# Starting every large on-chip tile of a decoder trunk at a multiple of 256 bytes

## The chip, the cores and the metric

The kernel runs on one core of a Trainium2 chip. The metric is the time of one execution on the device in microseconds (us), the median of three runs. A profile is one more execution, taken by the hardware profiler.

## What is computed

One decoder layer over 512 tokens of width 1024, all in float32, and a final norm. Cut to what matters here:

```python
h = rmsnorm(x, norm1_g)
x_rnn, g_rnn, dq, dk, dv, fq, fk, fv, f_logit, gates = split(h @ w_in)      # 1024 x 8200
y_rnn = gelu(g_rnn) * rg_lru(causal_conv4(x_rnn))                           # width 1024
lam   = exp(sum(lq1 * lk1)) - exp(sum(lq2 * lk2)) + 0.2                     # one number
y_diff = rmsnorm(diff_attention(dq, dk, dv, lam, rel_bias)) * 0.8           # 4 heads
y_fox  = forgetting_attention(fq, fk, fv, cumsum(log_sigmoid(f_logit + b))) # 8 heads
m = sum_b sigmoid(gates_b) * (y_b @ w_branch_b)
x = x + m @ w_out
u_gate, u_val = split(causal_conv3(rmsnorm(x, norm2_g) @ ffn_up))           # 1024 x 5632
x = x + (gelu(u_gate) * u_val) @ ffn_down                                   # 2816 x 1024
out = rmsnorm(x, final_g)
```

## The kernel before

Every product is a sum of three matmuls: each float32 operand is split into a high part `h` (rounded to the type float32r) and the rest `l`, and `mm3` (L81) adds h·h, h·l and l·h in a PSUM bank. A matmul reads two tiles of SBUF: the stationary one, 128 columns wide, which a weight load (PEld in the profile) puts into the array ahead of the matmul, and the moving one, as a rule 512 float32 columns (2,048 bytes in each partition). The TensorE (PE) has 4,363 matmuls, nearly all from the one line L77, and each has its own weight load.

Weights come from HBM in tiles of 128 x 1024. `load_w` (L93) puts one into a raw tile `wr`, ScalarE (ACT) casts it to `wh` (L101), VectorE (DVE) subtracts to get `wl` (L102). In the projections of the first half (`psq`, `psk`, `psx`, `psg`, `psgt`, and `psbr` for the branches) and in the FFN's first product (`psu`) `wh` and `wl` are the stationary side and an activation (`xh`/`xl`, `h2h`/`h2l`) moves; for one 128 x 512 result the order is sixteen matmuls with `wh` (each of its eight slices twice), then eight with `wl`. In the FFN's second product (`psd`) `wh`/`wl` move and the activations `acth`/`actl` are stationary. Its last weights on each half are held as pages (`wph`, `wpl`, from `load_wp`), and the product with w_out (`pswo`) moves `woh`/`wol`.

SBUF is divided into pools, laid one after the other: `const` (constants, each as long as it is), `page` (58 tiles of 2,048 bytes a partition, where most activations live), `wpool` (`wr`, `wh`, `wl`, three buffers each), `sm` (small vectors), and `apool`, which `fpool` follows in the same place (22 tiles of 2,048 bytes, for attention, later for `woh`/`wol` of the first five slices and for `acth`/`actl` of the first ten blocks). Where a pool starts follows from the length of those before it, and no pool is padded. A weight tile has 1,056 columns, since one pair of weights needs them; that is 4,224 bytes, 16 and a half times 256, so of three buffers in a row the middle one stands 128 bytes off the other two. In the built program the tiles start at these bytes past a multiple of 256:

- pages: 32
- `wr`: 32, 160, 32 (three buffers); `wh`: 160, 32, 160; `wl`: 32, 160, 32
- attention tiles: 96

Within a tile, slices start at multiples of 512 bytes, and so keep the tile's remainder.

A scheduler orders each engine's instructions when the kernel is built; an engine runs its own list in order and waits there. SyncE (SP) issues nearly all transfers. The first half interleaves eight heads of one attention and four of the other with the projections; from 475 us on the program is five long stretches, each of one kind of matmul.

Two constants matter for the change. `rows` (L160) holds the forget bias (8 columns) and the four lambda vectors (256 columns), read from HBM by one transfer at L226. `bneg` (L252) is a 4 x 128 fill of -1e30, written to a scratch tensor at L256.

Of the kernel before, what the change touches and what calls it, by code (L numbers as in the profile page):

```python
# [10 lines left out]
F32 = mybir.dt.float32  # L11
F32R = mybir.dt.float32r
AF = mybir.ActivationFunctionType
ALU = mybir.AluOpType
ADD, SUB, MUL, MAX = ALU.add, ALU.subtract, ALU.mult, ALU.max
# [9 lines left out]
NPG = 58  # L25
NAT = 22
NWARM = 9
NLAST = (2, 4)
LAM_INIT = 0.2
GELU_C = 0.7978845608028654  # L30
# [7 lines left out]
    COFF[_n] = _o  # L38
    _o += _w
NCOL = _o  # L40
ROFF = {"fbf": 0, "lam": 8}
NROW = 264

T_XR, T_GR, T_DQ, T_DK, T_FQ, T_FK, T_GT = 0, 8, 16, 20, 24, 28, 32

# [1 line left out]
def build(ctx, tc, A, out):  # L47
    nc = tc.nc
    PE, V, SC, G = nc.tensor, nc.vector, nc.scalar, nc.gpsimd

    const = ctx.enter_context(tc.tile_pool(name="const", bufs=1))
    page = ctx.enter_context(tc.tile_pool(name="page", bufs=NPG))
    wpool = ctx.enter_context(tc.tile_pool(name="wpool", bufs=3))
# [7 lines left out]
    def pg(name, dt=F32):  # L61
        return page.tile([128, 512], dt, name=name, tag="pg")

    def ag(name, dt=F32):
        return apool[0].tile([128, 512], dt, name=name, tag="at")
# [4 lines left out]
    def abank(name):  # L70
        return psa.tile([128, 512], F32, name=name, tag="at")

    def small(shape, name, bufs=None):
        return sm.tile(shape, F32, name=name, tag=name, bufs=bufs)
# [16 lines left out]
    hp = [False]  # L91

    def load_w(ap, n, parts=1):  # L93
        raw = wpool.tile([128, 1056], F32, name="wr", tag="wr")
        hi = wpool.tile([128, 1056], F32R, name="wh", tag="wh", bufs=3)
        lo = wpool.tile([128, 1056], F32R, name="wl", tag="wl", bufs=3)
        with tc.high_priority() if hp[0] else ExitStack():
            for p in range(parts):
                c = slice(n // parts * p, n // parts * (p + 1))
                nc.sync.dma_start(raw[:, c], ap[:, c])  # L100
                SC.copy(hi[:, c], raw[:, c])  # L101
                V.tensor_sub(lo[:, c], raw[:, c], hi[:, c])  # L102
        return hi, lo

    def load_wp(ap):

        raw = wpool.tile([128, 1056], F32, name="wr", tag="wr")
        nc.sync.dma_start(raw[:, :1024], ap)
        res = []
        for p in range(2):  # L110
            c = slice(512 * p, 512 * (p + 1))
            h = pg("wph", F32R)
            l = pg("wpl", F32R)
            SC.copy(h, raw[:, c])
            V.tensor_sub(l, raw[:, c], h)
            res.append((h, l))
        return res
# [39 lines left out]
    V.memset(epsc, EPS)  # L157
    pre = const.tile([128, 1], F32, name="pre")
    SC.activation(pre, epsc, AF.Exp)
    rows = const.tile([128, NROW], F32, name="rows")  # L160

    def col(n, j, w=1):
        return cols[:, COFF[n] + j:COFF[n] + j + w]
# [4 lines left out]
    pw = abank("pwarm")  # L168
    for _ in range(NWARM):
        PE.matmul(pw, warm[:, 0:128], warm, start=True, stop=True)  # L170
# [19 lines left out]
    for w in range(KD // 2):  # L190
        load_x(2 * w)
        hi, lo = load_w(A["wv_d"][w], 1024, 2)
        load_x(2 * w + 1)
        if w == 0:
            nc.sync.dma_start(cols[:, 8:], A["cols"][:, 8:])
        todo = [(t, 2 * w + kk, j) for kk in range(2) for j in range(3) for t in range(NT)]
        if w == KD // 2 - 1:
            todo.sort()
        for t, k, j in todo:
            kk = k % 2  # L200
            a, b = ((xh[k], hi), (xl[k], hi), (xh[k], lo))[j]
            mm(pst[t], a[:, 128 * t:128 * (t + 1)], b[:, 512 * kk:512 * (kk + 1)],
               k == 0 and j == 0, k == KD - 1 and j == 2)

    ss1 = const.tile([128, 2, NT], F32, name="ss1")
    for t in range(NT):
        for hf in range(2):
            xt = ag("xt")
            nc.sync.dma_start(xt, A["x"][128 * t:128 * (t + 1), 512 * hf:512 * (hf + 1)])
            SC.activation(xt, xt, AF.Square, accum_out=ss1[:, hf, t:t + 1])  # L210
    pre_w = [load_w(A["w_t"][i], 1024) for i in (T_DQ, T_DK)]
    ssum = small([128, NT], "ssum", 1)
    V.tensor_add(ssum, ss1[:, 0, :], ss1[:, 1, :])
# [9 lines left out]
    nc.sync.dma_start(flip, A["flip"])  # L223
    flr = const.tile([128, 128], F32R, name="flr")
    V.tensor_copy(flr, flip)
    nc.sync.dma_start(rows, A["rows"].partition_broadcast(128))  # L226
    relb = const.tile([32, 4], F32, name="relb")
    nc.sync.dma_start(relb, A["rel_bias"])
    oh = ag("oh")[0:32, :]
# [19 lines left out]
    PE.matmul(bps[0:4, :], relb, oh, start=True, stop=True)  # L249
    bsb = ag("bsb")[0:4, :]  # L250
    V.tensor_copy(bsb, bps[0:4, :])
    bneg = const.tile([4, 128], F32, name="bneg")  # L252
    V.memset(bneg, NEG)
    bdr = dram.tile([4, 640], F32, name="bdr")
    nc.sync.dma_start(bdr[:, 0:512], bsb)
# [3 lines left out]
    def vload_t(ap, kper, n):  # L259
        return lambda: [load_w(ap[0], kper * n), load_w(ap[1], kper * n)]  # L260
# [14 lines left out]
    def ev_fv(g):  # L275
        def ev(t, ps):
            p = pg("fv", F32R)

            pv = p.rearrange("p (u x d) -> p u x d", u=2, x=4)
            src = ps[:, 0:256].rearrange("p (u x d) -> p u x d", u=2, x=2)  # L280
            with tc.high_priority():
                for x in range(2):
                    h = pv[:, :, 3 * x, :]
                    l = pv[:, :, 1 + x, :]
                    SC.activation(h, src[:, :, x, :], AF.Copy, scale=rs1[:, t:t + 1])
                    V.scalar_tensor_tensor(l, src[:, :, x, :], rs1[:, t:t + 1], h, op0=MUL, op1=SUB)
            fv[t][g] = p
            if g == 0:
                V.scalar_tensor_tensor(flog[:, t, :], ps[:, 256:264], rs1[:, t:t + 1],
                                       rows[:, ROFF["fbf"]:ROFF["fbf"] + 8], op0=MUL, op1=ADD)  # L290
        return ev


# [13 lines left out]
        slabs.append(tl)  # L307


    lamw = rows[:, ROFF["lam"]:ROFF["lam"] + 256].rearrange("p (a b) -> p a b", a=4)  # L310
    lamp = ag("lamp")[:, 0:128].rearrange("p (a b) -> p a b", a=2)
    V.tensor_mul(lamp, lamw[:, 0::2, :], lamw[:, 1::2, :])
    lams = small([128, 2], "lams", 1)
    V.tensor_reduce(lams, lamp, axis=mybir.AxisListType.X, op=ADD)
    lame = small([128, 2], "lame", 1)
    SC.activation(lame, lams, AF.Exp)
# [489 lines left out]
    wo = [None] * KD  # L806

    def wo_load(k):
        raw = wpool.tile([128, 1056], F32, name="wr", tag="wr")
        nc.sync.dma_start(raw[:, :1024], A["w_out"][128 * k:128 * (k + 1), :])  # L810
        hl = []
        for hf in range(2):
            al = ag if k < 5 else pg
            h = al("woh", F32R)
            l = al("wol", F32R)
            SC.copy(h, raw[:, 512 * hf:512 * (hf + 1)])
            V.tensor_sub(l, raw[:, 512 * hf:512 * (hf + 1)], h)
            hl.append((h, l))
        wo[k] = hl
# [8 lines left out]
    for c in range(2, 8):  # L828
        last += gi(2, c)
        if c < 7:  # L830
            last += do(lambda c=c: wo_load(c - 2))
    for c in range(0, 8, 2):
        last += pi_(2, c)
        if c < 6:
            last += do(lambda c=c: wo_load(5 + c // 2))
# [9 lines left out]
    def up_w(idx, paged=False):  # L845
        if paged:
            pp = load_wp(A["up_t"][idx])
            return lambda k: tuple(x[:, 128 * (k % 4):128 * (k % 4 + 1)] for x in pp[k // 4])
        hi, lo = load_w(A["up_t"][idx], 1024)
        return lambda k: (hi[:, 128 * k:128 * (k + 1)], lo[:, 128 * k:128 * (k + 1)])  # L850
# [42 lines left out]
                V.scalar_tensor_tensor(h2l[k][:, ts_], src, col("g2", k), h2h[k][:, ts_], op0=MUL, op1=SUB)  # L893


    fwh = const.tile([128, 88], F32, name="fwh")
    for j in range(3):
        V.tensor_scalar(fwh[:, 22 * j:22 * (j + 1)], col("fw", 44 * j + 22, 22), 0.5, None, op0=MUL)
    V.tensor_scalar(fwh[:, 66:88], col("fb", 22, 22), 0.5, None, op0=MUL)
# [64 lines left out]
    for hf in range(2):  # L964
# [8 lines left out]

        nl = NLAST[hf]
        nxt = load_w(A["dn_t"][hf, 0], 1024)
        for p in range(NP - nl):
            hi, lo = nxt
            if p + 1 < NP - nl:
                nxt = load_w(A["dn_t"][hf, p + 1], 1024)
            else:  # L980
                held = [(p, load_wp(A["dn_t"][hf, p])) for p in range(NP - nl, NP)]
            for kk in range(2):
                for t in range(NT):
                    dmm(t, 2 * p + kk, hi[:, 512 * kk:512 * (kk + 1)], lo[:, 512 * kk:512 * (kk + 1)])
# [81 lines left out]
```

## Time and profile before

| | |
|---|---|
| median of three runs | 949.76 us (948.43 to 950.57) |
| the profiled execution, its own time | 949.56 us |
| its span, first to last instruction | 947.7 us |
| PE busy | 934.7 us, 99% of the span |
| VectorE, ScalarE, GpSimd busy | 631.7, 486.6, 112.4 us |
| granted TensorE clock, mean | 0.996 of full speed |
| read from HBM | 92.26 MB |

A matmul's duration in a row (389 to 404 ns for 512 columns) includes its filling and draining, which overlap the next matmul. What a matmul costs in a stream is the distance from its start to the next one's; the rows give it as a stretch divided by a count.

### The profile page before, as it was taken

Reading aid. Unit: us, or ns where it says so; the run is one execution under the profiler, and the core shown is the slowest. Engines: PE = TensorE matmul, PEld = TensorE weight load, DVE = VectorE, ACT = ScalarE, POOL = GpSimd, SP = SyncE. Lnnn points to the kernel's source line nnn. Section 1 sums busy time; section 2 is a strip of 40 time slices with the busy share of each in tenths; the row PEclk is TensorE's granted clock in tenths of the full one; section 3 lists DMA queues with packets and bytes.
Section 4 is the critical chain, followed back from the end, with each engine's and each line's share of the span. In section 5 each row is a group of like instructions: output and inputs, shape, how many; then the busy total and the mean of one; then the engine's idle time right before and its main releaser. Section 6 shows DMA issues by size and latency. Waiting matters only on the chain.

```text
span 947.7 us, 11817 instructions
## 1 busy us (share of the span) xinstructions
PE 934.7 (99%) x4363; PEld 770.7 (81%) x4363; DVE 631.7 (67%) x1207; ACT 486.6 (51%) x839; POOL 112.4 (12%) x85
## 2 busy tenths in 40 slices
PE   9999999999998999999999999999999999999997
PEld 6788888998886887888888889888888888888885
DVE  5779787777669889755566634877677677633323
ACT  7668776855474775434453344544444444422212
POOL 0022210200133253221210000000000000000000
PEclk9999999999999999999999999999999999999999
DMA  9622222232231323223253600323223222334112
GB/s 320 194 80 87 95 73 68 68 112 76 98 106 58 104 67 112 85 82 101 67 200 110 207 16 1 112 91 109 90 89 99 102 89 90 112 105 140 45 67 89
DMA packets 31433, 95.14 MB, mean 100 GB/s; under 512 B 3680, under 2 KB 5220, under 8 KB 31376
## 3 DMA queue, kind: packets, MB, share of 16 engines
q1 hardware_dynamic: 30800, 93.35, 29.2%
q10 hardware_dynamic: 576, 1.05, 0.3%
q8 instruction: 34, 0.56, 0.2%
q14 instruction: 23, 0.19, 0.1%
HBM read 92.26 MB, written 2.12 MB: 100 GB/s over the span
## 4 chain that ended last, share of the span: by engine, by line
PE 95%; DVE 3%; issue 1%; DMA 0%; ACT 0%; SPq 0%; POOLq 0%; POOL 0%
PE psu L77 26%; PE psgt L77 13%; PE psd L77 12%; PE psbr L77 9%; PE psg L77 6%; PE psv L77 5%; PE psx L77 5%; PE pswo L77 5%; PE psq L77 4%; PE psk L77 4%; PE pss L77 2%; PE pso L77 2%; PE pst L429 1%; DVE hh L637 1%; DVE gr L638 1%
## 5 line engine op out<-in xcount | busy, mean ns | idle before, releaser
L101 ACT CAST wh<-wr 128x1024 fp32r<-128x1024 f32 (+2 forms) x143 | 146.4, 1024 | 157.0 <-PE psu L77 55.3
L102 DVE TENSOR_TENSOR wl<-wr,wh 128x1024 fp32r<-128x1024 f32 (+2 forms) x143 | 174.1, 1217 | 75.3 <-ACT wh L101 66.7
L77 PE MATMUL psu<-h2l,wh 128*128 128x512 f32 (+1 forms) x360 | 136.9, 384 | 0.0
L77 PE MATMUL psu<-h2h,wh 128*128 128x512 f32 (+1 forms) x360 | 136.9, 383 | 0.0
L77 PE MATMUL psu<-h2h,wl 128*128 128x512 f32 (+1 forms) x360 | 87.2, 384 | 0.0
L77 PEld LDWEIGHTS psu<-h2l,wh 128*128 128x128 f32 x360 | 67.8, 188 | 14.0
L77 PEld LDWEIGHTS psu<-h2h,wh 128*128 128x128 f32 x360 | 67.8, 188 | 13.8
L77 PEld LDWEIGHTS psu<-h2h,wl 128*128 128x128 f32 x360 | 65.8, 188 | 14.4
L77 PE MATMUL psgt<-xh,wh 128*128 128x512 f32 x192 | 76.6, 399 | 0.0
L77 PE MATMUL psgt<-xl,wh 128*128 128x512 f32 x192 | 76.2, 397 | 0.0
L77 PE MATMUL psd<-wh,actl 128*128 128x512 f32 x128 | 50.2, 393 | 0.0
L77 PE MATMUL psd<-wl,acth 128*128 128x512 f32 x128 | 50.1, 391 | 0.0
L77 PE MATMUL psd<-wh,acth 128*128 128x512 f32 x128 | 49.9, 392 | 0.0
L77 PE MATMUL psgt<-xh,wl 128*128 128x512 f32 x192 | 49.1, 395 | 0.0
L864 POOL TENSOR_TENSOR rs3y<-rs3y,mhalf 128x1 f32<-128x1 f32 x4 | 2.2, 551 | 364.5 <-DVE rs3y L863 364.5
L77 PEld LDWEIGHTS psgt<-xh,wl 128*128 128x128 f32 x192 | 35.7, 188 | 8.1
L77 PEld LDWEIGHTS psgt<-xh,wh 128*128 128x128 f32 x192 | 36.1, 188 | 7.5
L77 PEld LDWEIGHTS psgt<-xl,wh 128*128 128x128 f32 x192 | 36.1, 188 | 7.5
L926 DVE SCALAR_TENSOR_TENSOR u<-gq,u 128x512 f32<-128x512 f32 x22 | 15.2, 692 | 34.1 <-ACT gq L925 34.1
L651 DVE TENSOR_TENSOR z<-psgt,rsb 128x512 f32<-128x512 f32 x24 | 16.5, 688 | 31.1 <-PE psgt L77 31.1
L906 DVE SCALAR_TENSOR_TENSOR u<-psu,cols,u 128x511 f32<-128x511 f32 (+1 forms) x44 | 32.9, 748 | 6.1 <-ACT u L903 5.3
L123 ACT CAST acth<-u 128x512 fp32r<-128x512 f32 x22 | 13.7, 621 | 43.5 <-DVE u L927 43.5
(288 smaller groups left out, 2179.6 us busy)
## 6 DMA issues: line engine op xcount, KB each, us to landing
wr<-w_t_in SPq DMA_DIRECT2D x56, 512.0 KB, 3.3
wr<-up_t_in SPq DMA_DIRECT2D x44, 512.0 KB, 3.3
wr<-dn_t_in SPq DMA_DIRECT2D x22, 512.0 KB, 3.4
wr<-br_r_in SPq DMA_DIRECT2D x8, 512.0 KB, 3.4
wr<-w_out_in SPq DMA_DIRECT2D x8, 512.0 KB, 3.9
xraw<-xT_in SPq DMA_DIRECT2D x8, 256.0 KB, 6.0
wr<-wv_d_in SPq DMA_DIRECT2D x8, 256.0 KB, 5.4
xt<-x_in SPq DMA_DIRECT2D x8, 256.0 KB, 5.4
```

The lines of the kernel that those rows point to most:

```text
L77: PE.matmul(ps, a, b, start=start, stop=stop)
L101: SC.copy(hi[:, c], raw[:, c])
L102: V.tensor_sub(lo[:, c], raw[:, c], hi[:, c])
L123: SC.copy(h, src)
L429: PE.transpose(ps[:, 128 * i:128 * (i + 1)], ws[i][:, 128 * j:128 * (j + 1)], ident)
L637: V.tensor_tensor_scan(hh, a, xc, 0.0, op0=MUL, op1=ADD)
L638: V.scalar_tensor_tensor(gr, gr, 0.5, hh, op0=MUL, op1=MUL)
L651: V.tensor_mul(z, ps, rsb)
L864: G.tensor_tensor(y, y, mhalf[:, 0:1], op=ALU.pow)
L906: V.scalar_tensor_tensor(u[:, s:], ps[:, :512 - s], w[j], u[:, s:], op0=MUL, op1=ADD)
L926: V.scalar_tensor_tensor(ug, q, 1.0, ug, op0=ADD, op1=MUL)
```

## The change

Lengths of tiles are changed so that every pool, and every tile in the pools `page`, `wpool` and `apool`/`fpool`, starts at a multiple of 256 bytes. In the built program all these tiles then stand at 0 past a multiple of 256, in place of 32, 96 and 160.

- Weight tiles get 1,088 columns (4,352 bytes, 17 times 256) in place of 1,056. The columns that are used stay the same.
- To make room, the 256 lambda columns leave `rows` and come by a transfer of their own into an attention tile `lamr`; the product of lambda vectors and `bneg` use other columns of the same tile.
- `fwh` and `lams` are made longer as padding; the added columns are not used.

No computing instruction is added or taken away; one transfer of 8 and one of 256 columns stand in for one of 264.

```diff
+WCOL = 1088
...
-ROFF = {"fbf": 0, "lam": 8}
-NROW = 264
+NFB = 8
...
-        raw = wpool.tile([128, 1056], F32, name="wr", tag="wr")
-        hi = wpool.tile([128, 1056], F32R, name="wh", tag="wh", bufs=3)
-        lo = wpool.tile([128, 1056], F32R, name="wl", tag="wl", bufs=3)
+        raw = wpool.tile([128, WCOL], F32, name="wr", tag="wr")
+        hi = wpool.tile([128, WCOL], F32R, name="wh", tag="wh", bufs=3)
+        lo = wpool.tile([128, WCOL], F32R, name="wl", tag="wl", bufs=3)
...
-    rows = const.tile([128, NROW], F32, name="rows")
+    rows = const.tile([128, NFB], F32, name="rows")
...
-    nc.sync.dma_start(rows, A["rows"].partition_broadcast(128))
+    nc.sync.dma_start(rows, A["rows"][0:NFB].partition_broadcast(128))
+    lamr = ag("lamr")
+    nc.sync.dma_start(lamr[:, 0:256], A["rows"][NFB:NFB + 256].partition_broadcast(128))
...
-    bneg = const.tile([4, 128], F32, name="bneg")
+    bneg = lamr[0:4, 384:512]
...
-    lamw = rows[:, ROFF["lam"]:ROFF["lam"] + 256].rearrange("p (a b) -> p a b", a=4)
-    lamp = ag("lamp")[:, 0:128].rearrange("p (a b) -> p a b", a=2)
+    lamw = lamr[:, 0:256].rearrange("p (a b) -> p a b", a=4)
+    lamp = lamr[:, 256:384].rearrange("p (a b) -> p a b", a=2)
...
-    lams = small([128, 2], "lams", 1)
+    lams = small([128, 24], "lams", 1)[:, 0:2]
...
-    fwh = const.tile([128, 88], F32, name="fwh")
+    fwh = const.tile([128, 144], F32, name="fwh")
```

The scheduler's lists differ in few places, all in the first 70 us or so; behind them PE, DVE, ACT and SP have the same lists as before. On SP, before, some 20 us into the execution (the constants and the relative bias table `relb`, its one-hot matrix `oh` and the scratch `bdr`):

```order
L223 DMA flip<-flip_in 128x128
L226 DMA rows<-rows_in 128x264
L228 DMA relb<-rel_bias_in 32x4
L230 DMA oh<-onehot_in 32x512
L256 DMA bdr<-bneg 4x128
L100 DMA wr<-w_t_in 128x1024 x4
```

and now:

```order
L223 DMA flip<-flip_in 128x128
L226 DMA rows<-rows_in 128x8
L228 DMA lamr<-rows_in 128x256
L230 DMA relb<-rel_bias_in 32x4
L232 DMA oh<-onehot_in 32x512
L258 DMA bdr<-lamr 4x128
L100 DMA wr<-w_t_in 128x1024 x4
```

One transfer more stands ahead of `relb`, `oh` and the weights. On DVE, before, at 26 to 42 us (`dvl` splits the first values, `bsb` takes the bias table out of PSUM, `hkl` splits its shifted copies, `lamp`, `lams` and `nlam` make lambda):

```order
L225 CAST flr<-flip 128x128
L102 TENSOR_TENSOR wl<-wr,wh 128x1024
L244 SCALAR_TENSOR_TENSOR dvl<-psv,rs_327,dvh 128x512 x2
L102 TENSOR_TENSOR wl<-wr,wh 128x1024
L251 COPY bsb<-bps 4x512
L244 SCALAR_TENSOR_TENSOR dvl<-psv,rs_327,dvh 128x512
L102 TENSOR_TENSOR wl<-wr,wh 128x1024
L124 TENSOR_TENSOR hkl<-hk,hkh 128x512 x4
L312 TENSOR_TENSOR lamp<-rows 128x128
```

and now:

```order
L225 CAST flr<-flip 128x128
L314 TENSOR_TENSOR lamr<-lamr 128x128
L102 TENSOR_TENSOR wl<-wr,wh 128x1024
L246 SCALAR_TENSOR_TENSOR dvl<-psv,rs_327,dvh 128x512
L316 TENSOR_REDUCE lams<-lamr 128x2
L246 SCALAR_TENSOR_TENSOR dvl<-psv,rs_327,dvh 128x512
L102 TENSOR_TENSOR wl<-wr,wh 128x1024
L253 COPY bsb<-bps 4x512
L246 SCALAR_TENSOR_TENSOR dvl<-psv,rs_327,dvh 128x512
L320 TENSOR_TENSOR nlam<-lame 128x1
L321 TENSOR_SCALAR nlam<-nlam 128x1
```

The four small operations of lambda come ahead of `bsb` and `hkl`; before, they came behind. PE, before, at 40 to 48 us (`psj` are the bias slabs, put between the matmuls of a projection `psx`):

```order
L77 MATMUL psj<-hkl,flr 128x512
L77 MATMUL psj<-hkh,flr 128x512
L77 MATMUL psx<-xl,wh 128x512
L77 MATMUL psj<-hkl,flr 128x512
L77 MATMUL psj<-hkh,flr 128x512
L77 MATMUL psx<-xh,wh 128x512
```

The change puts the first pair of `psj` two matmuls of `psx` later and the last pair behind the sixteenth:

```order
L77 MATMUL psx<-xl,wh 128x512
L77 MATMUL psx<-xh,wh 128x512
L77 MATMUL psx<-xl,wh 128x512
L77 MATMUL psj<-hkl,flr 128x512
L77 MATMUL psj<-hkh,flr 128x512
L77 MATMUL psx<-xh,wl 128x512 x8
```

## Rows read from the trace of the kernel before

**Rows 1.** The page: busy time, share of span, instructions; chain by engine.

```profile
PE 934.7 (99%) x4363; PEld 770.7 (81%) x4363; DVE 631.7 (67%) x1207; ACT 486.6 (51%) x839; POOL 112.4 (12%) x85
...
PE 95%; DVE 3%; issue 1%; DMA 0%; ACT 0%; SPq 0%; POOLq 0%; POOL 0%
```

**Rows 2.** PE's waits over the span: for whom, us, times, longest.

```profile
PE psbr L77 <- DVE xs L587: 3.4, 1, 3.4
PE pwarm L170 <- POOL warm L167: 1.3, 1, 1.3
PE psv L77 <- ACT wh L101: 0.8, 1, 0.8
```

**Rows 3.** PE's timeline in three neighbouring psu results: start, length, what, count.

```profile
597.91 0.39 PE L77 MATMUL psu<-h2h,wh 128*128 128x512 f32 x1
...
601.54 2.03 PE L77 MATMUL psu<-h2h,wl 128*128 128x512 f32 x8
603.41 0.40 PE L77 MATMUL psu<-h2h,wh 128*128 128x512 f32 x1
...
607.13 1.99 PE L77 MATMUL psu<-h2h,wl 128*128 128x512 f32 x8
608.97 0.40 PE L77 MATMUL psu<-h2h,wh 128*128 128x512 f32 x1
...
612.70 2.02 PE L77 MATMUL psu<-h2h,wl 128*128 128x512 f32 x8
614.55 0.39 PE L77 MATMUL psu<-h2h,wh 128*128 128x512 f32 x1
```

**Rows 4.** The chain that ended last, 921 to 935 us: start, us, what.

```profile
920.78 14.29 PE psd L77 x63
```

**Rows 5.** The same chain over the whole span, its pieces from 474 us.

```profile
474.37 31.16 PE psgt L77 x135
505.54 22.15 PE psbr L77 x96
527.69 18.68 PE pswo L77 x81
...
574.49 5.50 PE psu L77 x46
...
580.86 239.11 PE psu L77 x1082
819.97 115.79 PE psd L77 x504
```

**Rows 6.** The same chain before 475 us: first two and last of sixteen pieces x24.

```profile
29.53 5.74 PE psq L77 x24
35.27 5.50 PE psk L77 x24
...
367.08 5.54 PE psq L77 x24
```

**Rows 7.** 512-column matmuls at 20 to 475 us: largest and smallest of 35 groups.

```profile
L77 PE MATMUL psgt<-xh,wh 128*128 128x512 f32 x151 | 60.5, 401 | 0.0
...
L77 PE MATMUL pso<-wth,dvl 128*128 128x512 f32 x4 | 1.6, 393 | 0.0
```

**Rows 8.** DVE's split of a block, activations at 96, then in pages (at 32): min/median/max.

```profile
L124 DVE TENSOR_TENSOR actl<-u,acth x10: 680/682/692, 601.6 to 696.0; 128x512 fp32r<-128x512 f32 x10
L124 DVE TENSOR_TENSOR actl<-u,acth x9: 691/693/693, 728.6 to 817.4; 128x512 fp32r<-128x512 f32 x9
```

**Rows 9.** SP's timeline, 19 to 31 us.

```profile
19.83 0.33 SPq L226 DMA_DIRECT2D rows<-rows_in  x1
20.52 0.34 SPq L228 DMA_DIRECT2D relb<-rel_bias_in  x1
21.20 0.32 SPq L230 DMA_DIRECT2D oh<-onehot_in  x1
```

**Rows 10.** `oh`'s transfer and user; then lambda's first operations on DVE.

```profile
L249 PE MATMUL bps<-oh,relb x2: 587/587/587, 28.5 to 28.9; 32*4 32x512 f32 x2
...
DMA to landing us min/median/max: 5.5/5.5/5.5
...
L312 DVE TENSOR_TENSOR lamp<-rows x1: 284/284/284, 40.6 to 40.6; 128x128 f32<-128x128 f32 x1
L314 DVE TENSOR_REDUCE lams<-lamp x1: 277/277/277, 41.4 to 41.4; 128x2 f32<-128x128 f32 x1
```

More of the change, by code (lines that the diff above doesn't have):

```diff
@@ L105, in load_wp @@
     def load_wp(ap):
-        raw = wpool.tile([128, 1056], F32, name="wr", tag="wr")
+        raw = wpool.tile([128, WCOL], F32, name="wr", tag="wr")
         nc.sync.dma_start(raw[:, :1024], ap)
@@ L289, in ev @@
                 V.scalar_tensor_tensor(flog[:, t, :], ps[:, 256:264], rs1[:, t:t + 1],
-                                       rows[:, ROFF["fbf"]:ROFF["fbf"] + 8], op0=MUL, op1=ADD)
+                                       rows, op0=MUL, op1=ADD)
         return ev
@@ L808, in wo_load @@
     def wo_load(k):
-        raw = wpool.tile([128, 1056], F32, name="wr", tag="wr")
+        raw = wpool.tile([128, WCOL], F32, name="wr", tag="wr")
         nc.sync.dma_start(raw[:, :1024], A["w_out"][128 * k:128 * (k + 1), :])
```

## The prediction

> **What bounds the kernel now.** I read the page first. PE is busy for 99% of the span and makes 95% of the chain that ended last; VectorE makes 3% of it, and transfers almost nothing [rows 1]. The list of waits agrees: PE waits in full view only three times for more than 0.7 us, once for 3.4 us behind a late VectorE chain [rows 2]. So time can only come from what a matmul itself costs, and the next question is whether that is a constant. It is not.
>
> The timeline of three neighbouring results of `psu` shows it [rows 3]. All three do the same: sixteen matmuls with `wh` stationary, eight with `wl`, on the same moving pages. In the first, the sixteen take 601.54 - 597.91 = 3.63 us, 226.9 ns each. In the second they take 607.13 - 603.41 = 3.72 us, 232.5 ns each, and in the third 612.70 - 608.97 = 3.73 us, 233.1 ns. All that differs in PE's operands is which of the three `wh` buffers is read. By the built program the first result has the middle buffer, which starts 32 bytes past a multiple of 256, as the moving pages do; the other two have buffers at 160. The `wl` tiles lie the other way round, and so does their time: the first result's eight, at 160, take 603.41 - 601.54 = 1.87 us (233.8 ns), the second's, at 32, 608.97 - 607.13 = 1.84 us (230.0 ns).
>
> The best stretch of the whole execution is the end of `psd`, where moving (`wph`, `wpl`) and stationary tiles (`acth`, `actl`) are all pages: 63 matmuls in 14.29 us, 226.8 ns each [rows 4]. Nowhere else does a long stretch come that low. The other long pieces of the chain [rows 5] are mixtures: `psgt` 31.16 / 135 = 230.8 ns, `psbr` 230.7 ns, `psd` as a whole 229.7 ns. So I read from the rows: **a 512-column matmul costs 226.8 ns when its moving and stationary tile have the same remainder to 256, and some 230 to 233 ns when they have not.** The clock is no part of this: the granted share is full in all these stretches (226.8 ns is 544 cycles of the upper level, 2.4 GHz; 512 columns alone would be 213.3 ns).
>
> **The change, part by part.**
>
> *All large tiles at remainder 0.* Then every pair of moving and stationary tile has equal remainders. I take 226.8 ns for a 512-column matmul in a stream. From the pieces behind 474 us [rows 5], what each gives back:
>
> - `psgt`: 31.16 - 135 x 0.2268 = 0.54 us
> - `psbr`: 22.15 - 96 x 0.2268 = 0.38 us
> - `pswo`: the piece with 81 costs 230.6 ns each; 192 in all (eight results of 24) x 3.8 ns = 0.73 us
> - `psu`: of 1,082 matmuls 98 have 256 columns. The piece of 46 before it is only of those, 5.50 / 46 = 119.6 ns each, so they take 11.72 us and the other 984 take 227.39 us, 231.1 ns each. They give 227.39 - 223.17 = 4.22 us
> - `psd`: 115.79 - 504 x 0.2268 = 1.48 us
>
> Together 7.3 us. In these stretches PE never waits for long, the order is unchanged and the runs are hundreds of matmuls long, so I count it whole.
>
> Between 20 and 475 us, 1,653 matmuls of 512 columns run (the sum of 35 groups, from x151 to x4) [rows 7]. The sixteen unbroken pieces of 24 of them take 5.56 us on average (5.74 and 5.50 to 5.54 in the rows), 231.6 ns each [rows 6]. At 226.8 ns each the 1,653 would give 4.8 ns x 1,653 = 7.9 us. Not all of it comes. A matched stream doesn't start at 226.8 ns: the second result's `wl` group above was matched, and its eight still took 1.84 us instead of 1.81, so getting into step cost some 0.026 us [rows 3]. In this stretch transposes, scores and value products of other lengths cut the projections into pieces; by the timeline there are some 130 runs and another 50 breaks by waits. About 180 x 0.026 = 4.7 us if each pays in full; many are too short to pay it all, so I take 3.9 and keep 4.0 us. The bounds are 0 (each run always out of step) and 7.9 us.
>
> Matmuls of 256, 264 and 384 columns I leave as they are: 119.6 ns in an unbroken piece whose tiles match in part already [rows 5]. No row shows them all matched; the bound is 256 columns at the upper level, 106.7 ns, for some 350 of them: 4.5 us, which the range's lower end does not count.
>
> *What VectorE and ScalarE do with the new addresses.* VectorE shows a small effect with the other sign: the same split takes 682 ns with activations at 96 and the source at 32, and 693 ns with all at 32, 1.6% more [rows 8]. If every VectorE operation paid that, its 631.7 us would grow by 10 us [rows 1], nearly all hidden under PE. What shows is its 3% of the chain, 28 us: 0.45 us. The nearer bound is 0, since part of its operands match already; I take 0.4, and that also covers what the VectorE-bound pieces swallow of PE's gain ahead of them.
>
> *The extra transfer.* SP issues a transfer in 0.33 us and one every 0.68 us here [rows 9], so `relb`, `oh` and the next weights go out 0.7 us later. `oh` lands 5.5 us after its issue at 21.20, at 26.7 us, and its user starts at 28.5 us [rows 10]: 1.8 us of cover hide it. Without that cover it would cost 0.7 us. The bias table's and `bneg`'s transfers are behind it on the same queue and are needed later still.
>
> *Lambda ahead of `bsb` and `hkl` on VectorE.* Product and reduction are 0.28 us each [rows 10], and the two operations of `nlam` are smaller. They delay the bias table by less than 1 us, and with it the four pairs of `psj`, behind which the rest of `psx` stands in PE's list. The list now puts the first pair two matmuls (0.46 us) later. Between 0 and 0.7 us; I take 0.2. Moving `lame` ahead of the casts on ScalarE costs 0.2 us of an engine that is 51% busy [rows 1]. `bneg` in the same tile, padding of `fwh` and `lams`: nothing, no operation grows.
>
> **Sum** against the profiled execution's own 949.56 us: 949.56 - 7.3 - 4.0 + 0.4 + 0.2 = 938.9 us. That execution is 0.2 us under the median of the runs, so I say 939 us, 1.1% faster. A difference of 0.2% (1.9 us) is about what a measurement of this kernel can tell from none.
>
> **The rivals.**
>
> *Only the five long stretches gain.* In the first half the runs never fall into step, or the gain turns into waits for VectorE, which is the chain's only other large engine. Then 949.6 - 7.3 = 942.3 us. For it: short runs and the 3.4 us wait. Against it: unbroken pieces of 24 there already reach 5.50 us (229 ns) while two thirds of their tiles do not match.
>
> *Nothing changes.* What I read as equal remainders could be something else that goes with the middle buffer, its absolute place for one; then the stream stays at 229 to 231 ns and the time at 949.7 us. Against it: `wl`, whose middle buffer is the unmatched one, shows the opposite order, and pages matched with pages are the best of all. The Trainium skill has a rule that points this way: "SBUF — State Buffer", in the section on Door 1, says that SBUF works in lines of 16 bytes, and that an access pays when it crosses to a new line; 32, 96, 160 and 0 are all whole lines, so by it alone the change is worth nothing. The 5.6 ns between the buffers [rows 3] disagree with that as a full account.
>
> *Slower.* Remainder 0 may be a bad one: if both tiles start at the edge of the same 256-byte line, their reads could collide at every line, and every 512-column matmul could cost what the worst stretch costs now, 232.5 to 233 ns [rows 3]. At 232.5, `psu` loses 1.4 us, `psd` 1.4, the other three 0.9, the first half 0.9 ns x 1,653 = 1.5: together 5.2 us, 954.8 us. It decides from a mean of about 231 ns upward. For it: no tile stands at 0 today, so no row shows that case. Against it: equal remainders of 32 collide just as much in principle and are the best.
>
> *Much faster.* All starts today are 32 past a multiple of 64. If the 13.5 ns that a matched matmul costs above 213.3 ns come from that, they could go as well: some 3,560 matmuls (the 1,653 and 1,911 in the five stretches) x 13.5 ns = 48 us more, 891 us. The Trainium skill, "TensorE: Matmul & The Clock Gate", section "Wait — 56ns, not 53.3ns?", gives 215.7 ns for back-to-back matmuls of 512 columns at the upper clock; no row here comes near it, the lowest long stretch being 226.8 [rows 4], so that overhead is hardly a matter of remainders alone.
>
> **Chances.** The forecast 0.64, only the long stretches 0.16, nothing 0.07, slower 0.08, much faster 0.05. The range takes in the first two with their bounds: low, with the whole 7.9 us of the first half, 949.6 - 15.2 = 934 us; high, with half of the 7.3 us and nothing else, 946 us. That holds 0.80. Faster by over 0.2%: 0.64 + 0.16 + 0.05 = 0.85. The same 0.07, slower 0.08.
>
> **What would show it.** In the profile after: three neighbouring `psu` results take 24 x 226.8 ns = 5.44 us each, without the pattern of three; the `psu` piece of the chain falls to about 235 us and `psd` to 114.3; pieces of 24 in the first half come to 5.45 to 5.52 us; VectorE's busy time grows by 0 to 10 us; the waits of PE before 50 us grow by no more than 0.7 us. The prediction is wrong if a long stretch settles elsewhere than at 226.8 ns, or if the first half's PE time is regained by idle time before `psbr`, `pso` or `pss`.

## The result, and the profile after

The changed kernel takes 939.02 us (median of four runs, 938.27 to 939.65) against 950.16 us for the kernel before in the same comparison: a ratio of 0.9886, 95% interval 0.9869 to 0.9903. The profiled execution took 939.65 us, its span 937.9 us. The page of the changed kernel, busy time of each engine:

```profile
PE 925.1 (99%) x4363; PEld 771.2 (82%) x4363; DVE 632.2 (67%) x1207; ACT 486.4 (52%) x839; POOL 111.0 (12%) x85
```

Against [rows 1], PE is busy 9.6 us less in a span that is 9.8 us shorter, with as many matmuls; no other engine's busy time moved by more than 1.4 us. The chain that ended last, after the change (start, us, what, count), answers to [rows 5], and its first pieces show the start:

```profile
5.94 24.08 PE psv L77 x96
30.46 0.95 PE bps L251 x2
...
471.86 30.63 PE psgt L77 x135
502.48 21.76 PE psbr L77 x96
524.24 18.37 PE pswo L77 x81
...
576.93 234.82 PE psu L77 x1082
811.75 114.25 PE psd L77 x504
```

The five long pieces lost 0.5, 0.4, 0.3, 4.3 and 1.5 us. From 474.37 us to the end the kernel before took 473.3 us; from the same matmul, now at 471.86 us, it takes 466.0 us: 7.3 us. PE's timeline over three results of `psu` shows why, as [rows 3] did before:

```profile
597.61 1.98 PE L77 MATMUL psu<-h2h,wl 128*128 128x512 f32 x8
...
603.05 1.98 PE L77 MATMUL psu<-h2h,wl 128*128 128x512 f32 x8
...
608.49 1.98 PE L77 MATMUL psu<-h2h,wl 128*128 128x512 f32 x8
```

Each result now takes 603.05 - 597.61 = 5.44 us, like the next (608.49 - 603.05), 24 x 226.7 ns; the pattern of three is gone. In the first half the pieces of 24 on the chain went from [rows 6] to these (first, second and last of sixteen):

```profile
31.40 5.67 PE psq L77 x24
37.08 5.44 PE psk L77 x24
...
365.81 5.49 PE psq L77 x24
```

Their mean is 5.47 us (228.0 ns for each matmul) where it was 5.56. The waits of PE stayed as they were: 3.4 us for `psbr` [rows 2], 0.7 for `pso`, none new.

### The profile page after: what moved, and what is told of

Its sections match the earlier page's. It is cut to its first block, busy times and chain, and to the rows that moved or that the text cites. A ratio compares the mean times of both kernels' runs of the same rounds, so it can differ in the third digit from the quotient of the medians.

```text
span 937.9 us, 11818 instructions
## 1 busy us (share of the span) xinstructions
PE 925.1 (99%) x4363; PEld 771.2 (82%) x4363; DVE 632.2 (67%) x1207; ACT 486.4 (52%) x839; POOL 111.0 (12%) x85
## 4 chain that ended last, share of the span: by engine, by line
PE 95%; DVE 3%; issue 1%; DMA 0%; ACT 0%; SPq 0%; POOLq 0%; POOL 0%
PE psu L77 26%; PE psgt L77 13%; PE psd L77 12%; PE psbr L77 9%; PE psg L77 6%; PE psv L77 5%; PE psx L77 5%; PE pswo L77 5%; PE psq L77 4%; PE psk L77 4%; PE pss L77 2%; PE pso L77 2%; PE pst L431 1%; DVE hh L639 1%; DVE gr L640 1%
```

## The experiments

Theory A: a float32r matmul of 512 columns depends on the difference of the remainders (to 256 bytes) of its moving and its stationary tile, and is at its best when they are equal. Theory B: multiples of 256 are good by themselves. Where a layer kernel is edited, the edit is to the changed kernel, and PE's list stays the same word for word (two of them have a fill of an extra padding tile on VectorE, and their line numbers are three higher).

**The pairs by themselves (m1).** A kernel of matmuls alone: two tiles that start at multiples of 256, and 26 pairs of starts inside them.

```diff
+PAIRS = [(0, 0), (4, 4), (16, 16), (32, 32), (96, 96), (128, 128), (0, 4), (0, 16), (0, 32), (0, 64), ...]
+        a = st[:, s // 4:s // 4 + 128]
+        b = mv[:, m // 4:m // 4 + 512]
+        for j in range(N):
+            PE.matmul(bank, a, b, start=j == 0, stop=j == N - 1)
```

> Only matmuls: 26 groups of 40 matmuls of 512 float32r columns from two tiles, each group with its own start (stationary, moving) in bytes past a multiple of 256; nothing of the layer is computed. Theory A (only the difference of the two remainders counts): 226.7 ns start to start for the equal pairs 0/0, 4/4, 16/16, 32/32, 96/96, 128/128 and for differences of 256, 512, 1024; about 229 ns at a difference of 64, about 232 ns at 128. Theory B (the place of a tile against the 256-byte line counts by itself, whatever the other tile's): 0/0 is the lowest, and 96/96 and 128/128 cost 230 ns or more. Theory C (what looked like remainders was other traffic of the layer): all groups cost the same.

PE's timeline of that kernel, one row for a group of 40 (start, length, what); the groups shown are 0/0, 4/4, 16/16, 32/32, 96/96, 128/128, then, stationary first, 0/4, 0/64, 0/96, 0/128, 0/160, 0/256, 0/512, 64/0 and 128/0:

```profile
16.25 9.24 PE L44 MATMUL pa<-mv,st 128*128 128x512 f32 x40
25.33 9.67 PE L44 MATMUL pb<-mv,st 128*128 128x512 f32 x40
34.83 9.37 PE L44 MATMUL pc<-mv,st 128*128 128x512 f32 x40
44.04 9.27 PE L44 MATMUL pd<-mv,st 128*128 128x512 f32 x40
53.15 9.28 PE L44 MATMUL pe<-mv,st 128*128 128x512 f32 x40
62.27 9.26 PE L44 MATMUL pf<-mv,st 128*128 128x512 f32 x40
71.36 9.63 PE L44 MATMUL pg<-mv,st 128*128 128x512 f32 x40
...
99.43 9.31 PE L44 MATMUL pj<-mv,st 128*128 128x512 f32 x40
108.58 9.49 PE L44 MATMUL pk<-mv,st 128*128 128x512 f32 x40
117.91 9.49 PE L44 MATMUL pl<-mv,st 128*128 128x512 f32 x40
127.24 9.53 PE L44 MATMUL pm<-mv,st 128*128 128x512 f32 x40
...
164.61 9.25 PE L44 MATMUL pq<-mv,st 128*128 128x512 f32 x40
173.70 9.23 PE L44 MATMUL pr<-mv,st 128*128 128x512 f32 x40
...
201.16 9.48 PE L44 MATMUL pu<-mv,st 128*128 128x512 f32 x40
210.48 9.46 PE L44 MATMUL pv<-mv,st 128*128 128x512 f32 x40
```

Divide the distance from one row's start to the next by 40. 0/0: (25.33 - 16.25) / 40 = 227.0 ns. 32/32, 96/96 and 128/128: 227.8, 228.0 and 227.3, the first few matmuls of each group being slower until the stream is in step. 0/256: 227.3. With the moving tile 64 past the stationary one it is 228.8; 96 past, 233.3; 128 past, 233.3. Theory B and the theory of other traffic in the layer fall: 96/96 is as good as 0/0, and the pattern stands in a kernel without any other work. Theory A holds, but with a limit that it did not foresee: 4/4 takes 237.5 ns and 16/16 takes 230.3, so equal remainders are good among the multiples of 32 that were tried.

**All tiles at 32 (e1).** The layer again, with all large tiles 32 bytes past a multiple of 256.

```diff
-    fwh = const.tile([128, 144], F32, name="fwh")
+    fwh = const.tile([128, 152], F32, name="fwh")
```

> The changed kernel with 32 bytes more of padding ahead of the pages, so that pages, weights and attention tiles all start at 32 past a multiple of 256; the instruction lists are the same. Theory A: as the changed kernel, 939 us within 1 us, psu piece 235 us. Theory B (multiples of 256 are good by themselves): back toward the kernel before, 945 to 950 us. If the transfers of the first 20 us gain from aligned ends, their rate falls from 406 to about 390 GB/s here, and the time rises by no more than 1 us.

937.79 us, ratio 0.9867 (0.9853 to 0.9882). Its chain:

```profile
5.93 22.08 PE psv L77 x96
...
574.92 234.81 PE psu L77 x1082
809.74 114.25 PE psd L77 x504
```

The five long pieces are those of the changed kernel to 0.01 us, with no large tile at a multiple of 256. Theory B is out. The total is 1.2 us under the changed kernel's, a little more than the 1 us expected; the first 96 matmuls alone differ by 2.0 us (22.08 against 24.08), and e7 and e8 ask why.

**Pages 128 off (e2).**

```diff
-    fwh = const.tile([128, 144], F32, name="fwh")
+    fwh = const.tile([128, 176], F32, name="fwh")
...
+    padp = ctx.enter_context(tc.tile_pool(name="padp", bufs=1))
+    padt = padp.tile([128, 32], F32, name="padt")
+    nc.vector.memset(padt, 0.0)
     wpool = ctx.enter_context(tc.tile_pool(name="wpool", bufs=3))
```

> The changed kernel with the pages at 128 and weights and attention tiles at 0: every tile still a multiple of 128, but projections, psu, most of psbr and pswo and the later half of psd read two tiles whose remainders differ by 128. Theory A: 232.4 ns in the psu stretch, its piece about 241 us, in all 954 to 957 us, slower than both kernels. Theory B: 128 is half as good as 0, between 940 and 948 us, psu piece under 238 us.

953.27 us, ratio 1.0037 (1.0024 to 1.005): slower than the kernel before, though every large tile stands at a multiple of 128. The chain:

```profile
585.55 240.30 PE psu L80 x1082
```

That is 5.5 us more in `psu` than in the changed kernel, from an offset alone. Both the total and `psu` came out 0.7 us under what theory A gave.

**Pages 64 off (e3).** As e2, with 160 columns for `fwh` and 48 for `padt`.

```diff
-    fwh = const.tile([128, 144], F32, name="fwh")
+    fwh = const.tile([128, 160], F32, name="fwh")
```

> The changed kernel with the pages at 64 and weights and attention tiles at 0. Theory A with the costs of single pairs measured before (moving 64 past the stationary tile: 228.9 ns, 64 short of it: 233.3 ns): psu piece 237.0 us; psd 117 us, since its later activations are pages at 64 under weights at 0; in all 946 to 949 us. Rival (any two multiples of 64 are as good as equal): 939 us.

947.85 us, ratio 0.9978 (0.9964 to 0.9991), and on the chain:

```profile
580.82 236.64 PE psu L80 x1082
817.46 115.33 PE psd L80 x504
```

`psu` is 0.4 us from what the single pairs of m1 said, `psd` 1.7 us under what was expected. In its trace the price is there, 233.3 ns, but for some 160 of the 504 matmuls alone ((115.33 - 114.25) us / 6.6 ns); the others read two tiles of one remainder, among them the last ones, whose tiles are all pages. With the moving tile past the stationary one, an offset of 64 costs a third of what 128 costs in `psu`; two multiples of 64 are not as good as equal.

**The weights' length alone undone (e4).** Pages and attention tiles stay at 0 (`lams` makes up for the pool's length); two of three `wh` buffers and one of three `wl` buffers stand 128 off again.

```diff
-WCOL = 1088
+WCOL = 1056
...
-    lams = small([128, 24], "lams", 1)[:, 0:2]
+    lams = small([128, 56], "lams", 1)[:, 0:2]
```

> The changed kernel with weight tiles of 1,056 columns again, pages and attention tiles still at 0: two of three wh buffers and one of three wl buffers are 128 off the pages. Theory A: the pattern of three comes back in psu, its piece 239 us, psgt's 31.1 us; psd and pswo keep part of the gain; in all 947 to 949 us. Rival (the gain comes from the pools' places or from the moved constants, not from the weight tiles' length): 939 to 941 us.

949.79 us, ratio 0.9995 (0.9985 to 1.0005), no different from the kernel before. The chain:

```profile
528.64 18.36 PE pswo L77 x81
...
581.35 239.11 PE psu L77 x1082
820.46 115.81 PE psd L77 x504
```

`psu` has the 239.11 us of [rows 5] to the last digit; only `pswo`, which reads no such tile, kept its gain. `psd` kept none, against the expectation: its moving tiles are the weights. The total is 0.8 us above the expected range. In the profiled execution, 1.2 us of the first half has another cause. Right behind PE's 3.4 us wait for `psbr` the granted clock stands at 0.50, the lower level, from 292.4 to 299.2 us, 6.8 us long; e2's trace has such a stretch too, and those of the other layer kernels, the kernel before's included, have one of 3.4 us.

**The moved constants alone (e5).** The instruction lists of the changed kernel, all addresses as before.

```diff
-WCOL = 1088
+WCOL = 1056
...
-    lams = small([128, 24], "lams", 1)[:, 0:2]
+    lams = small([128, 2], "lams", 1)[:, 0:2]
...
-    fwh = const.tile([128, 144], F32, name="fwh")
+    fwh = const.tile([128, 472], F32, name="fwh")
```

> The changed kernel's instruction lists (the split transfer of constants, lambda and the fill in the attention tile) with all addresses as in the kernel before: weight tiles of 1,056 columns, pages at 32, attention tiles at 96. Theory A (the whole gain comes from addresses): 949.5 to 951 us, the same as before. Rival (the moved constants or the new order in the first 70 us give part of it, or cost something): 1 us or more away from the kernel before.

949.85 us, ratio 0.9997 (0.9987 to 1.0006). The extra transfer and the new order neither give nor cost anything that shows; the interval leaves room for about 1 us, but the trace is narrower: from `bps` to the long `psgt` piece e5 takes 445.6 us, the kernel before 445.8.

**The attention pool alone at 96 (e6).**

```diff
-    lams = small([128, 24], "lams", 1)[:, 0:2]
+    lams = small([128, 48], "lams", 1)[:, 0:2]
```

> The changed kernel with the attention pool alone at 96, pages and weights at 0. Theory A: psd's first 240 matmuls of each pair of halves meet activations at 96 under weights at 0 (234.4 ns where stationary stands 96 past moving), pswo's first five slices move at 96 over pages at 0 (233.3 ns): psd about 116 us, pswo up by 0.8 us, the attention products by some 0.3 us, in all 941 to 942.5 us. Rival (only the weight tiles' length counts): 938 to 939.5 us. The rate of transfers at 10 to 20 us should fall below 406 GB/s if it goes by the attention tiles' starts.

941.17 us, ratio 0.9905 (0.9889 to 0.9922), and on the chain:

```profile
523.04 18.85 PE pswo L77 x81
...
811.52 116.12 PE psd L77 x504
```

`psd` and the longest piece of `pswo` rise by 1.9 and 0.5 us (`pswo` by 1.0 us in all, where 0.8 was expected); `psu` and `psgt` do not move. So the pool's place is worth about 2 us, once the weights are matched.

**What is left of a matched matmul (m2).** Matmuls alone, with other shapes and in bf16; the bf16 rows below list 39 of their 40.

```diff
+PAIRS = [("r", 128, 512, 0, 0), ("r", 64, 512, 0, 0), ("r", 32, 512, 0, 0), ("r", 16, 512, 0, 0), ...]
+        a = ts[:, s // w:s // w + mc]
+        b = tm[:, m // w:m // w + nc_]
```

> Only matmuls again, nothing of the layer: 18 groups of 40, in float32r and bf16, with 128 to 16 stationary columns, 512 to 256 moving columns, and remainders 0/0 or unequal. The question is where the 13.3 ns (32 cycles of the upper clock level) come from that a matched matmul costs above 512 columns. Theory D (the next weight load takes a turn from the moving stream for every 4 of its columns, 16 bytes): 226.7 ns with 128 stationary columns, 220.0 with 64, 216.7 with 32; 384 moving columns take 173.3 ns and 256 take 120.0 ns matched. Rival (a fixed cost for each matmul): 226.7 ns whatever the stationary columns. For bf16, whose columns are 2 bytes: 220 ns by theory D if the turns go by 16 bytes, and a smaller or no effect of unequal remainders.

Its timeline: float32r with 128 and 64 stationary columns, and the start of the group behind them; with 384 and 256 moving ones, first matched (`pe`, `pf`), then with the moving tile 128 past the stationary one (`pg`, `ph`); then bf16 at 0/0, 0/32 and 0/64:

```profile
15.71 9.23 PE L52 MATMUL pa<-mv,st 128*128 128x512 f32 x40
24.77 9.36 PE L52 MATMUL pb<-mv,st 128*64 128x512 f32 x40
33.97 9.43 PE L52 MATMUL pc<-mv,st 128*32 128x512 f32 x40
...
52.51 7.12 PE L52 MATMUL pe<-mv,st 128*128 128x384 f32 x40
59.47 4.95 PE L52 MATMUL pf<-mv,st 128*128 128x256 f32 x40
64.25 7.20 PE L52 MATMUL pg<-mv,st 128*128 128x384 f32 x40
71.30 4.90 PE L52 MATMUL ph<-mv,st 128*128 128x256 f32 x40
76.03 8.81 PE L52 MATMUL pi<-mvb,stb 128*128 128x512 bf16 x39
84.68 8.80 PE L52 MATMUL pj<-mvb,stb 128*128 128x512 bf16 x39
93.31 8.79 PE L52 MATMUL pk<-mvb,stb 128*128 128x512 bf16 x39
```

Matched float32r takes 226.5 ns with 512 moving columns (9.06 us / 40), 174.0 with 384 and 119.5 with 256: 30 to 34 cycles of 2.4 GHz above the columns each time, as theory D has it. But 64 stationary columns take 230.0 ns (9.20 us / 40), more and not less, so theory D's account of the 32 cycles falls, and so does the rival of a fixed cost. bf16 takes 216.3 ns (8.65 us / 40) at 0/0 and 215.8 (8.63 us / 40) at 0/32, where theory D had 220: unequal remainders cost bf16 nothing here. The Trainium skill, "TensorE: Matmul & The Clock Gate", section "Wait — 56ns, not 53.3ns?", gives 215.7 ns, and these rows agree.

m2 also shows where matching float32r tiles does not pay. At 128 off, 384 moving columns take 176.3 ns (7.05 us / 40), 2.3 more than matched, but 256 take 118.3 (4.73 us / 40), 1.2 less than matched. With 64 stationary and 512 moving columns it is (155.29 - 146.12) / 40 = 229.3 ns at 128 off and 230.0 matched. So the rule is shown for 128 stationary columns and for 512 and 384 moving ones.

**The two good kernels side by side (e7, e8).** The changed kernel and e1, unedited, on one chip.

> The changed kernel once more, beside the kernel with all tiles at 32, on one chip. Theory A: both take the same long stretches, psu 234.8 us and psd 114.3 us. If the 1.9 us that the profiled execution of the changed kernel lost before 31 us belong to the clock's state at its start and not to the addresses or the extra transfer, its first stretch of 96 matmuls takes about 22.1 us when the first matmuls start at the upper level, and the medians of the two kernels lie within 1 us of each other. If the addresses at 0 cost it, that stretch takes 24 us again and the changed kernel stays 1 to 2 us behind.

> All tiles at 32 once more, beside the changed kernel: 937.5 to 939.5 us by either theory; the comparison with the changed kernel on the same chip is what tells.

938.87 us (ratio 0.9876, 0.9859 to 0.9892) and 938.96 us (0.9874, 0.9857 to 0.9891): the same. This time it was the kernel with tiles at 32 whose profiled execution began slowly, its first 96 matmuls taking 23.78 us from 6.20 us on, against 22.79 us for the changed kernel, whose first four were slow too. The slow start goes with the execution and not with these two kernels' addresses: each of the two took longer in one execution (24.08 and 23.78 us) than in the other (22.79 and 22.08).

## Why the prediction was right, point by point

**What bounds it, and the rule.** Right. PE was the bound, and the remainder pattern that the three `psu` results showed is the cause: m1 has it without the layer, e1 keeps the gain with no large tile at a multiple of 256, e2 loses it with every tile at a multiple of 128, and e4 takes the whole gain back by the weight tiles' length alone.

**The five long stretches: 7.3 us.** Measured 7.3 us. Four of the five terms are within 0.1 us of their working; `pswo` gave 0.5 us where it had 0.73, since its shorter pieces on the chain (37, 20 and 17 matmuls) come to 227.6 to 229.4 ns and not to 226.8. Matmuls of 256 columns, which were left out, gave nothing: the piece of 46 in `psu` went from 5.50 [rows 5] to 5.51 us.

**The first half: 4.0 us kept of 7.9, less 0.4 and 0.2.** From `bps`, at 28.59 us on the chain of the kernel before ([rows 10] have it at 28.5), to 474.37 us [rows 5] it was 445.8 us; now it is 441.4 us, from 30.46 to 471.86. That is 4.4 us where the terms sum to 3.4. Pieces of 24 came to 228.0 ns, 0.03 us above 24 x 226.8, so the price of one run was about what I took (0.026 us); it is their total of 3.9 us that was too large, and how many runs paid it was not measured. No wait grew.

**VectorE: 0.4 us.** This step failed, harmlessly. I read the 682 and 693 ns of [rows 8] as an effect of remainders. With all tiles at 0 the split still differs; VectorE's rows after the change, early blocks and then late ones:

```profile
L124 DVE TENSOR_TENSOR actl<-u,acth x10: 681/683/693, 597.6 to 690.3; 128x512 fp32r<-128x512 f32 x10
L124 DVE TENSOR_TENSOR actl<-u,acth x9: 691/692/693, 722.2 to 809.3; 128x512 fp32r<-128x512 f32 x9
```

So it goes with the pool the tile is in, or with the time, and not with the remainder. What it is stays open. VectorE's busy time grew by 0.5 us in all.

**The extra transfer and the order: 0.2 us.** Nothing to be seen in e5, to 0.2 us.

**The start, which had no term.** The kernel reached `bps` 1.9 us later in this execution. PE's timeline of the changed kernel:

```profile
5.94 2.07 PE L77 MATMUL psv<-wh,xh 128*128 128x512 f32 x4 [0.57 <-ACT wh L101]
7.81 1.91 PE L77 MATMUL psv<-wh,xl 128*128 128x512 f32 x4
9.52 1.45 PE L77 MATMUL psv<-wl,xh 128*128 128x512 f32 x4
```

and of e1, which has the same lists:

```profile
5.93 1.20 PE L77 MATMUL psv<-wh,xh 128*128 128x512 f32 x4 [0.96 <-ACT wh L101]
6.97 1.08 PE L77 MATMUL psv<-wh,xl 128*128 128x512 f32 x4
7.89 1.08 PE L77 MATMUL psv<-wl,xh 128*128 128x512 f32 x4
```

Four matmuls from 7.81 to 9.52 us are 427 ns each, what 512 columns take at the lower clock level, 1.2 GHz; in e1 they are 230 ns. The windows of the profile read a granted share of 1.00 there, but only because the trace's records of the granted clock begin later. The first record, of the upper level, begins at 10.28 us in the changed kernel, at 9.94 in e8 and at 7.33 in e7, and at 4.44 and 4.50 us in e1 and the kernel before: in each where its matmuls become fast. So it was the clock. Ahead of it stand, in both kernels shown, the nine warm-up matmuls and an idle time of 0.6 or 1.0 us; why the rise came later in some executions stays open. It made the 96 matmuls 2.0 us longer than e1's.

That the median fell on the forecast is therefore in part luck: in the profiled execution the first half gave 1.0 us more than its terms, and the start, which had none, took the 1.9 us back.

**The rivals.** "Only the five long stretches gain" did not happen, the first half kept 4.4 us. Its argument that two thirds of the tiles do not match holds for `wh` alone: with `wl` it is 40 of the 72 matmuls of three results. "Nothing changes" is refuted by the result, and by m1, where 0/0 and 0/96 differ by 6 ns; 4/4 and 16/16 show that something below 32 bytes counts too. The rule of 16-byte lines that the prediction takes from the Trainium skill ("SBUF — State Buffer", Door 1) is no full account by these rows. "Slower" named the wrong place: remainder 0 is as good as 32. Its price for `psu` was close, 1.2 us lost in e2 where it had 1.4, but `psd`, of which e2 unmatches a part alone, lost nothing (115.25 us), so that e2's 953.27 us beside its 954.8 is no test of the sum, whose three small stretches come to 0.8 and not 0.9 us. "Much faster" is refuted for float32r: being at a multiple of 64 brought nothing below 226.5 ns.

## What to carry to other kernels

When PE is the bound, divide a long stretch by its matmuls and compare it with the best stretch in the same trace; a pattern that repeats with the number of weight buffers points at addresses. Give the moving and the stationary tile of a float32r matmul of 512 columns, with 128 stationary ones, the same remainder to 256 bytes: every buffer's length a multiple of 256, and the pools' starts alike (0 and 32 were as good in the layer, 96 and 128 too in m1). In this kernel that was worth 1.1% for no computing instruction at all, and one buffer length of 1,056 columns was enough to lose all of it.

## What the hardware showed that I had not expected

- The difference has a sign. A matmul takes 228.8 ns with the moving tile 64 bytes past the stationary one (m1, 0/64), and (210.48 - 201.16) / 40 = 233.0 ns with the stationary one 64 bytes past the moving one (64/0). Why unequal remainders cost time at all, no run shows.
- Where the 32 cycles of a matched float32r matmul come from is open. They do not shrink with fewer stationary columns (m2), and bf16 has only some 6 or 7 of them.
- Transfers in the loaded stretch from 10 to 20 us ran faster in the changed kernel. The stretch's rows (busy time of the engines, granted clock, share of the transfer engines, GB/s) of the kernel before, then of the changed one:

```profile
10.00:20.00 10.00, 10.00 (x45) 8.13 (x45) 8.61 (x26) 9.68 (x20) 0.00 (x0) 1.00 1.05 391
```

```profile
10.00:20.00 10.00, 10.00 (x45) 8.28 (x44) 8.77 (x27) 9.91 (x21) 0.00 (x0) 1.00 1.05 406
```

That is 4% more; e1 and e8 (tiles at 32) have 390 and 391, e5 (32, 96, 160) 392, e2, e4 and e7 (weights and attention tiles at 0 or 128) 406 to 408; e3 and e6 lie between with 397 and 402, so the starts are not the whole account. It brought no time, since PE was not waiting for these transfers.
